# mLSTM values leave their PSUM banks into the tiles of the mLSTM's loads: a decoder block on one core

## The chip, the cores and the metric

The kernel runs on one NeuronCore of a Trainium2 chip, as one program. Five engines work side by side, each through its own queue of instructions: TensorE (PE) multiplies matrices into banks of PSUM, VectorE (DVE) and ScalarE (ACT) work elementwise and read PSUM, GpSimd (POOL) works on SBUF and issues transfers, SyncE (SP) issues transfers. The engines wait for each other by semaphores. The metric is the device time of one execution in microseconds (us).

## What is computed

One decoder block over a sequence of 2048 tokens of width 1024, in float32. Two token mixers run in parallel on one combined projection, followed by a gated FFN:

```python
h = modulate(rms_norm(x, g_pre_mix[l]), shift_m, scale_m)
proj = h @ w_in[l]
q_a, k_a, v_a, q_m, k_m, v_m, o_m, i_m, f_m, g_a, g_m = jnp.split(proj, split_points, axis=-1)
...
y_a = sliding_window_attention(q_a, k_a, v_a, attn_sinks[l]).astype(x.dtype)
...
h_m = mlstm_chunkwise(q_m.reshape(B, S, MLSTM_HEADS, MLSTM_HEAD_DIM),
                      k_m.reshape(B, S, MLSTM_HEADS, MLSTM_HEAD_DIM),
                      v_m.reshape(B, S, MLSTM_HEADS, MLSTM_HEAD_DIM), i_pre, f_pre)
y_m = (jax.nn.sigmoid(o_m.astype(jnp.float32)) * head_layer_norm(h_m, mlstm_norm_w[l])).astype(x.dtype)
merged = jax.nn.sigmoid(g_a) * (y_a @ w_branch_attn[l]) + jax.nn.sigmoid(g_m) * (y_m @ w_branch_mlstm[l])
mix = merged @ w_out[l]
x = x + gate_m[:, None, :] * rms_norm(mix, g_post_mix[l])
h2 = modulate(rms_norm(x, g_pre_ffn[l]), shift_f, scale_f)
ff = (jax.nn.silu(h2 @ w_ffn_gate[l]) * (h2 @ w_ffn_up[l])) @ w_ffn_down[l]
x = x + gate_f[:, None, :] * rms_norm(ff, g_post_ffn[l])
```

Here `v_m`, the mLSTM's values, are 512 columns of the projection (4 heads of 128). They are what the change is about.

## The kernel before

**Tiling.** The sequence is cut into four blocks of 512 tokens (`TB`, numbered 0 to 3), and each block into four token tiles of 128 (`NT`). Two blocks make a superblock: blocks 0 and 1, then blocks 2 and 3. Each matrix product is made of three matmuls per operand pair, since each float32 operand is split into a high and a low part (`mm3`, line 283; ScalarE casts the high part, VectorE subtracts the low part: lines 267 and 268 or 1744 and 1745). The larger products of the projection go by a seven-product scheme over two blocks at once (`pair_parts`, line 1854).

**Stages of a superblock.** The projection goes in this order (`superblock`, line 769): for the first block the attention's queries, then keys, values and mLSTM gates, then the mLSTM's values (`vm`, line 867); for the second block keys and values first, then queries, then the mLSTM's values; then for both blocks the pairs of output gate, mLSTM queries and keys, and branch gates. In block 0 the first products are made by `first_block` in an order written out by hand. Attention, the gates' scan and later the mLSTM's chunks run as streams: Python generators that are spawned with a due time and stepped between matmuls (`tick`, line 231), so their instructions lie between those of the projection.

**A product by token groups.** `token_group` (line 339) takes four PSUM banks, one for each token tile (`acc_tile`, a pool of four banks), and goes through the weights two rows of tiles at a time. In the last step it finishes token tile 0, hands its bank to `evac`, then token tile 1, and so on. The next group takes the same four banks in the same order, so its first matmul into a bank follows the evacuation of that bank.

**The values.** `evac` in `vm` (lines 868 to 871) takes a tile, copies the bank into it on ScalarE (line 870), and stores it to the DRAM tensor `vm_d` by a transfer that SyncE issues (line 871). The mLSTM's chunks read `vm_d` later (line 1084). There are four blocks with four token tiles each: 16 copies and 16 stores.

**The two pools of tiles in question.** `tx` (line 124) gives tiles of a pool with nine buffers, the common temporaries. Its other users around the values are: the copies of the queries' banks and their rotated form (lines 813 and 787), the keys and values of blocks 1 to 3 (line 839) and their rotated form, the pieces of the adaLN weights that SyncE loads (line 475 and 476), and the results of the pairs. A query's or key's tile is given back when its stores to `at_d` have landed, which POOL issues (lines 806, 833, 851 and 853). `ld` (line 735) gives tiles of a pool with four buffers. Its users are the keys and values of block 0 (line 839; the stores of lines 851 and 853 and the transpose of line 827 read them) and the loads of the mLSTM's keys and queries by chunk (line 1078, two tiles for a chunk). A tile is 128 partitions by 512 float32 in both. A user that finds no free buffer waits for the last reader of the oldest one.

**Order.** `first_block` is in program order on the engines. After it (line 1713) the framework's planner, with a simulated time line (`schedule_with_timeline_sim=True`, line 2237), orders each engine's queue at compile time: an instruction whose tile is not yet free in the simulation can be placed behind others that the program lists later. On the chip each engine then takes its queue in that order.

**Lines that are named further on.** Line 212 is every matmul of a product, line 217 every transpose. Lines 569, 575 and 576 reload and split the input's combinations (`hsums`, line 564), lines 985 and 987 copy and mask the attention's scores, line 803 scales the transposed queries, line 829 copies the transposed keys, line 954 loads an attention block's operands, lines 333 and 1908 load weights. Line 90 stands for every instruction of the hand-written part.

Of the kernel before, what the change touches and what calls it, by code (L numbers as in the profile page):

```python
# [19 lines left out]
P = 128  # L20
# [53 lines left out]
def decoder_block(ctx: ExitStack, tc: tile.TileContext, a: dict, out: bass.AP, dbg=None):  # L74
# [39 lines left out]
    def nm(s):  # L114
        uid[0] += 1
        return f"{s}{uid[0]}"
# [7 lines left out]
    def tx(shape, dtype=F32):  # L124
        return tpool.tile(shape, dtype, tag="tx", name=nm("tx"), bufs=9)
# [192 lines left out]
    def kept_weights(name):  # L318

        n = 528 if name == "kv" else 1024  # L320
        for j0 in range(0, 4, 2):
            for j in ((j0,) if name == "kv" else (j0, j0 + 1)):
                def load(j=j):
                    src = W_D[name]
                    if name != "kv" and j % 2:
                        parts = [split_tile(x) for x in ("whi", "wlo")]
                        for i in range(2):
                            nc.sync.dma_start(parts[i].bitcast(F32), src[:, j, i, :])
                        return [parts]
                    m = 2 if name == "kv" else 1  # L330
                    t = wpool.tile([P, RAWC], F32R, tag="raw", name=nm("raw"))
                    v = t[:, :m * 2 * n].rearrange("p (m i c) -> p m i c", m=m, i=2)
                    nc.sync.dma_start(v.bitcast(F32), src[:, j:j + m, :, :])
                    return [[v[:, q, i, :] for i in range(2)] for q in range(m)]
                raw = Raw(load)
                for q in range(2 if name == "kv" else 1):
                    yield raw, q, 2 * (j + q), 2

    def token_group(srcs, nk, n, lhs, evac, pair_heads=False, stagger=1, store=None, kept=False):

        acc = []
        srcs = list(srcs)
        held = []

        def make(si, k0, kc):
            def mms(wt):
                if not acc:
                    acc.extend(acc_tile() for _ in range(NT))
                held.append((wt, k0, kc))
                if len(srcs) - stagger <= si < len(srcs) - 1:  # L350
                    return
                for t in range(NT):
                    for w_, k0_, kc_ in held:
                        for j in range(kc_):
                            kk = k0_ + j
                            mm3(acc[t][:, :n], lhs(kk, t), (w_[0][:, j, :], w_[1][:, j, :]), kk == 0, kk == nk - 1)
                            yield
                    if si == len(srcs) - 1:
                        evac(t, acc[t])
                held.clear()  # L360
            return mms

        for si, (raw, view, k0, kc) in enumerate(srcs):
            if kept:
                def ready(raw=raw, q=view):
                    return tuple(v.rearrange("p (k c) -> p k c", k=2) for v in raw.tile[q])
                yield Part(raw, ready, make(si, k0, kc))
                continue
            part = piece(raw, view, [kc, n], make(si, k0, kc), pair_heads)
            if store:  # L370
                def prep(do=part.prep, si=si, kc=kc):
                    made = do()
                    for i, v in enumerate(made):
                        nc.sync.dma_start(W_D[store][:, si, i, :].rearrange("p (k c) -> p k c", k=kc), v.bitcast(F32))
                    return made
                part.prep = prep
            yield part

    def srcs_rows(w, nk, c0):
        for k0 in range(0, nk, 4):  # L380
            kn = min(4, nk - k0)
            raw = raw_rows(w, k0, kn, c0)
            for j in range(0, kn, 2):
                yield raw, (lambda t, j=j: t[:, j:j + 2, :]), k0 + j, 2
# [350 lines left out]
    def ld(shape, dtype=F32):  # L735
        t = kvp.tile([P, 512], dtype, tag="ld", name=nm("ld"), bufs=4)
        return t.rearrange("p (k c) -> p k c", k=shape[0])
# [31 lines left out]
    def superblock(sb):  # L769
# [3 lines left out]
        def lhs_h(b):  # L773
            def lhs(kk, t):
                return tuple(p_[:, kk % 4, t * P:(t + 1) * P] for p_ in HC[f"{kk // 4 + 1}{b % 2 + 1}"])
            return lhs
# [89 lines left out]

        def vm(b):
            def evac(t, ps):
                v = tx([P, 512])
                A.copy(v, ps)  # L870
                nc.sync.dma_start(vm_d[b][:, t, :], v)
            if b > 1:
                yield from token_group(kept_weights("vm"), KD, 512, lhs_h(b), evac, kept=True)
            else:
                yield from token_group(srcs_rows(w_in, KD, C_VM), KD, 512, lhs_h(b), evac, store="vm" if b else None)
# [1379 lines left out]
```

## Time and profile before

| what | value |
| --- | --- |
| median of three runs | 2659.16 us (2657.73 to 2660.38) |
| the profiled execution, its own time | 2668.66 us |
| its span, first to last instruction | 2667.0 us |
| mean granted clock of TensorE | 0.994 |

All of the trace is from the one profiled execution. A row of a timeline gives the start and the length in us, the engine, the line of the kernel, the operation, what it writes and reads by the program's names, the shapes and how many were merged; in brackets stands how long the engine was idle before it, and what ended that wait. A row of a line gives the count, the shortest, median and longest duration in ns, and first and last start in us. `acc` and `mix` are PSUM banks, `tx` and `ld` tiles of the two pools, `hl`, `whi` and `wlo` split weights, `big` large tiles, `raw` weights as loaded. SPq and POOLq are the queues on which SyncE and POOL issue transfers.

### The profile page before, as it was taken

How to read it: one execution, taken by the hardware profiler on the slowest of the kernel's cores; microseconds unless marked ns; L12 is line 12 of the kernel's file. 1: busy time of each engine (PE TensorE's matmuls, PEld its weight loads, DVE VectorE, ACT ScalarE, POOL GpSimd, SP SyncE). 2: the span in 40 equal slices, each digit the busy share in tenths (PEclk: the TensorE clock that was granted, in tenths of full speed). 3: DMA queues.
4: the chain of work that ended last, by engine and by line, in shares of the span. 5: the costliest groups of instructions: out<-in, count | busy, mean ns of one | idle time of the engine just before them, and what ended most of it. 6: DMA issues, size and time to landing. Idle time of an engine off the chain costs nothing.

```text
span 2667.0 us, 36229 instructions
## 1 busy us (share of the span) xinstructions
PE 2615.5 (98%) x12546; PEld 2145.8 (80%) x12546; DVE 1937.2 (73%) x3758; ACT 1281.9 (48%) x2531; POOL 300.3 (11%) x473
## 2 busy tenths in 40 slices
PE   8999999999989999999999999999999999999998
PEld 6877788888876788888878888888778888888876
DVE  5878887768676988875777777775776767676466
ACT  6656544545654654454643433345554333333444
POOL 0320001101132000210001111110000011001000
PEclk9899999999999999999999999999999999999999
DMA  7785465887787545597765554446675323234556
GB/s 270 255 303 164 135 196 183 291 301 253 262 313 244 166 135 181 183 296 268 220 238 193 184 169 153 163 139 228 213 242 173 111 99 116 90 111 139 199 196 220
DMA packets 327032, 532.97 MB, mean 200 GB/s; under 512 B 23136, under 2 KB 197724, under 8 KB 320064
## 3 DMA queue, kind: packets, MB, share of 16 engines
q1 hardware_dynamic: 287752, 448.45, 50.4%
q0 software_dynamic: 20880, 66.41, 6.6%
q10 hardware_dynamic: 18216, 15.79, 1.9%
q8 instruction: 99, 1.62, 0.2%
q14 instruction: 85, 0.70, 0.1%
HBM read 367.61 MB, written 154.57 MB: 196 GB/s over the span
## 4 chain that ended last, share of the span: by engine, by line
PE 88%; DVE 4%; DMA 3%; ACT 2%; issue 1%; POOL 0%; ACTq 0%; SPq 0%; DVEq 0%; POOLq 0%
PE acc L212 62%; PE mix L212 22%; PE mix L217 2%; PE acc L90 1%; DVE hl L1745 1%; PE mix L90 1%; DMA raw<-as_d 1%; ACT hl L1744 1%; DMA big<-big 0%; DMA raw<-ws_d 0%; DMA raw<-in_w_in_dram 0%; ACT tm L1002 0%; DMA at_d<-tx 0%; DMA raw<-in_w_ffn_down_dram 0%; ACT big L575 0%
## 5 line engine op out<-in xcount | busy, mean ns | idle before, releaser
L212 PE MATMUL acc<-big,hl 128*128 128x512 f32 x3936 | 936.4, 393 | 7.0 <-ACT tx L870 5.4
L212 PEld LDWEIGHTS acc<-big,hl 128*128 128x128 f32 x3936 | 733.8, 188 | 166.4 <-ACT tx L870 5.9
L1744 ACT CAST hl<-raw 128x512 fp32r<-128x512 f32 x732 | 439.9, 621 | 489.6 <-PE acc L212 208.7
L1745 DVE TENSOR_TENSOR hl<-raw,hl 128x512 fp32r<-128x512 f32 x732 | 495.1, 692 | 198.4 <-ACT hl L1744 196.0
L212 PE MATMUL acc<-whi,big 128*128 128x512 f32 (+1 forms) x896 | 281.6, 390 | 3.0 <-ACT tx L870 3.0
L212 PE MATMUL mix<-big,hl 128*128 128x512 f32 x1056 | 263.0, 390 | 1.8 <-ACT hl L1744 1.1
L212 PE MATMUL acc<-hl,hl 128*128 128x512 f32 x1008 | 237.2, 393 | 6.2 <-DVE hl L1745 3.3
L212 PEld LDWEIGHTS mix<-big,hl 128*128 128x128 f32 x1056 | 197.8, 188 | 44.5 <-ACT hl L1744 2.0
L212 PEld LDWEIGHTS acc<-hl,hl 128*128 128x128 f32 x1008 | 187.1, 188 | 51.8 <-DVE hl L1745 8.8
L212 PEld LDWEIGHTS acc<-whi,big 128*128 128x128 f32 x896 | 168.6, 192 | 36.2 <-ACT tx L870 3.4
L212 PE MATMUL mix<-hl,hl 128*128 128x512 f32 x792 | 182.7, 391 | 3.4 <-ACT hl L1744 2.6
L212 PEld LDWEIGHTS mix<-hl,hl 128*128 128x128 f32 x792 | 147.8, 188 | 37.6 <-ACT hl L1744 4.2
L212 PE MATMUL acc<-wlo,big 128*128 128x512 f32 (+1 forms) x448 | 174.4, 389 | 0.0
L212 PE MATMUL acc<-big,whi 128*128 128x512 f32 x512 | 157.3, 393 | 0.0
L268 DVE TENSOR_TENSOR wlo<-raw,whi 128x1024 fp32r<-128x1024 f32 (+1 forms) x76 | 90.8, 1194 | 65.7 <-ACT whi L267 60.2
L267 ACT CAST whi<-raw 128x1024 fp32r<-128x1024 f32 (+1 forms) x76 | 78.4, 1032 | 109.7 <-PE acc L212 103.5
L492 POOL TENSOR_TENSOR rs<-ms,halves 128x1 f32<-128x1 f32 (+1 forms) x56 | 41.3, 744 | 797.8 <-DVE ms L490 750.4
L212 PE MATMUL mix<-hcT4h,hl 128*128 128x512 f32 x352 | 115.6, 389 | 0.7 <-ACT hl L1744 0.7
L212 PE MATMUL acc<-hcT2h,hl 128*128 128x512 f32 x352 | 115.5, 389 | 0.0
L212 PEld LDWEIGHTS acc<-big,whi 128*128 128x128 f32 x512 | 95.3, 188 | 19.3
L212 PEld LDWEIGHTS acc<-wlo,big 128*128 128x128 f32 x448 | 85.8, 192 | 18.0 <-issue 1.2
L212 PE MATMUL acc<-big,wlo 128*128 128x512 f32 x256 | 97.6, 392 | 0.0
(388 smaller groups left out, 3802.3 us busy)
## 6 DMA issues: line engine op xcount, KB each, us to landing
as_d<-w POOLq DMA_DIRECT2D x154, 256.0 KB, 2.5
raw<-in_w_in_dram SPq DMA_DIRECT2D x36, 1024.0 KB, 5.4
raw<-as_d SPq DMA_DIRECT2D x70, 512.0 KB, 3.8
raw<-in_w_ffn_gate_dram SPq DMA_DIRECT2D x22, 1024.0 KB, 6.1
raw<-in_w_ffn_up_dram SPq DMA_DIRECT2D x22, 1024.0 KB, 5.8
raw<-ws_d SPq DMA_DIRECT2D x40, 512.0 KB, 4.6
tx<-in_w_ada_dram SPq DMA_DIRECT2D x64, 256.0 KB, 5.3
g_d<-tx SPq DMA_DIRECT2D x64, 256.0 KB, 2.4
```

Of the source, the lines that this page charges most:

```text
L90: self.last = tc.keep_in_program_order(f(*p, **k)).ins
L212: T.matmul(o, lhsT=lhsT, rhs=rhs, start=start, stop=stop, skip_group_check=resumed)
L217: T.transpose(o, i, ident[:k, :k])
L267: A.copy(hv, src)
L268: V.tensor_tensor(lv, src, hv.bitcast(F32), op=ALU.subtract)
L492: G.tensor_tensor(r[:, :n], ms[:, :n], nhalf[:, :n], op=ALU.pow)
L1744: A.copy(v(hi), src)
L1745: V.tensor_tensor(v(lo), src, v(hi).bitcast(F32), op=ALU.subtract)
```

## The change

In `vm`, the tile into which a bank of values is copied comes from the pool of the mLSTM's loads, `ld`, in all four blocks. The copy and the store stay as they are.

```diff
         def vm(b):
             def evac(t, ps):
-                v = tx([P, 512])
+                v = ld([1, 512])[:, 0, :]
                 A.copy(v, ps)
                 nc.sync.dma_start(vm_d[b][:, t, :], v)
```

`ld` gives a tile of the same size as a view of three dimensions, so the index takes its one row:

```python
def ld(shape, dtype=F32):
    t = kvp.tile([P, 512], dtype, tag="ld", name=nm("ld"), bufs=4)
    return t.rearrange("p (k c) -> p k c", k=shape[0])
```

## The prediction

> **What bounds the kernel now.** I read the page first: its span, its busy times and its chain; then the windows, the rows of line 870, and the timelines around them.
>
> ```profile
> span 2667.0 us, 36229 instructions
> PE 2615.5 (98%) x12546; PEld 2145.8 (80%) x12546; DVE 1937.2 (73%) x3758; ACT 1281.9 (48%) x2531; POOL 300.3 (11%) x473
> ...
> PE 88%; DVE 4%; DMA 3%; ACT 2%; issue 1%; POOL 0%; ACTq 0%; SPq 0%; DVEq 0%; POOLq 0%
> ```
>
> TensorE is busy for 2615.5 of 2667.0 us, and the chain that ended last runs through it for 88% of the span. The change takes no matmul away, so it can gain only in the 51.5 us where TensorE stands. The windows show where that is (the stretch, its length, then busy time and count of PE, PEld, DVE, ACT and POOL, the granted clock, the DMA share and GB/s):
>
> ```profile
> 200.00:750.00 550.00, 549.79 (x2772) 457.30 (x2771) 425.56 (x915) 294.82 (x581) 58.38 (x68) 1.00 0.67 224
> 872.00:1370.00 498.00, 498.00 (x2455) 412.10 (x2455) 390.16 (x794) 266.84 (x520) 43.73 (x40) 1.00 0.63 207
> 1370.00:2667.00 1297.00, 1274.37 (x5609) 1043.73 (x5607) 894.56 (x1468) 539.45 (x985) 126.36 (x222) 1.00 0.50 168
> ```
>
> From 200 to 750 us TensorE stands 0.21 us in all, from 872 to 1370 not at all; there a faster copy is worth nothing. After 1370 runs the FFN, whose tiles come from a pool of its own. What is left lies before 200 us and between 750 and 872, and that is where line 870 runs:
>
> ```profile
> L870 ACT COPY tx<-acc x16: 575/587/596, 95.4 to 870.4; 128x512 f32<-128x512 f32 x16
> ...
>   PE acc L212: 8.4, 4
> ```
>
> TensorE waited for a copy of line 870 four times, 8.4 us in all. That is the whole direct prize, 0.3% of the span. These are the four (idle before, and who ended it, in brackets):
>
> ```profile
> 104.80 0.39 PE L212 MATMUL acc<-whi,big 128*128 128x264 f32 x1 [0.31 <-ACT tx L870]
> ...
> 108.97 0.59 PE L212 MATMUL acc<-whi,big 128*128 128x264 f32 x1 [2.69 <-ACT tx L870]
> ...
> 192.50 1.20 PE L212 MATMUL acc<-big,hl 128*128 128x512 f32 x4 [0.82 <-ACT tx L870]
> ...
> 858.72 1.22 PE L212 MATMUL acc<-big,hl 128*128 128x512 f32 x2 [4.55 <-ACT tx L870]
> ```
>
> Two fall in block 0, one in block 1, none in block 2, one in block 3.
>
> **The change part by part.** Nothing is added or taken away: 16 copies of 587 ns and 16 stores stay, source and shape are the same. What moves is the wait for a free tile: out of the nine common temporaries, into the four of the loads. So each block is asked the same question: does the load tile come free earlier, and what would TensorE wait for next?
>
> *Block 0.* The four load tiles hold the keys and values of block 0 here (line 839). ScalarE's rows:
>
> ```profile
> 98.17 0.63 ACT L267 CAST whi<-raw 128x528 fp32r<-128x528 f32 x1 [1.41 <-PE acc L212]
> 98.71 0.26 ACT L829 CAST tx<-mix 128x128 fp32r<-128x128 f32 x1
> 98.95 1.09 ACT L803 ACTIVATE tx<-mix 128x512 fp32r<-128x512 f32 x2
> 102.09 2.18 ACT L575 CAST big<-big 128x512 fp32r<-128x512 f32 x4 [2.05 <-DMA big<-big]
> 104.18 0.57 ACT L870 COPY tx<-acc 128x512 f32<-128x512 f32 x1
> 108.34 0.59 ACT L870 COPY tx<-acc 128x512 f32<-128x512 f32 x1 [3.58 <-issue]
> 108.82 1.21 ACT L985 COPY tm<-mix 128x256 f32<-128x256 f32 x4
> ```
>
> Copies three and four come at 104.18 and 108.34, behind work that the program lists after them; ScalarE stood 3.58 us before the fourth. The view names no releaser; below is a store of line 833 that landed 0.1 us before, and whose common tile a key stream gives back, so I take it for the one. The last reader of a load tile is line 851, the store of the value difference:
>
> ```profile
> L851 POOL DMA_DIRECT2D at_d<-ld x3: 540/540/549, 79.9 to 84.2; - x3
> ...
> DMA to landing us min/median/max: 2.0/3.0/3.0
> ```
> ```profile
> 98.73 0.73 POOL L833 DMA_DIRECT2D at_d<-tx  x1 [4.69 <-issue]
> 99.46 0.55 POOL L851 DMA_DIRECT2D at_d<-ld  x1
> ```
> ```profile
> L833 POOL DMA_DIRECT2D at_d<-tx x1: 729/729/729, 98.7 to 98.7; - x1
> ...
> DMA to landing us min/median/max: 9.5/9.5/9.5
> ```
> ```profile
> at_d<-ld POOLq DMA_DIRECT2D x1, 64.0 KB, 9.5
> ```
>
> That store of line 833 landed at 98.73 + 9.5 = 108.23. Three load tiles are free by 84.2 + 3.0 = 87.2 us, or once TensorE has transposed their keys, before the copies want them; so copies one to three go when their banks are full and the 0.31 us goes. The fourth load tile's store goes out at 99.46 and lands 9.5 us later, at 108.96. So the fourth copy exchanges one landing for the next one on the same queue, 0.73 us behind. Nothing covers that: TensorE stands from 108.97 - 2.69 = 106.28 for this copy alone. Behind it on ScalarE stand the four score copies of line 985, which move with it; their attention step follows TensorE's key group and shifts as that does. The end of the stall moves from 108.97 to about 109.7. **Block 0: +0.7 us**, the 0.31 us being swallowed by the longer wait behind it.
>
> [...]
>
> ```profile
> 92.00:112.00 20.00, 17.00 (x113) 15.29 (x112) 16.01 (x36) 10.64 (x22) 6.65 (x11) 0.90 0.96 334
> ```
>
> The DMA engines are 96% busy in these 20 us. I take the 9.5 us.
>
> *Block 1.* The load tiles stand idle here: their own loads begin at 374.6 us, and block 1's keys go through common temporaries.
>
> ```profile
> L1079 SPq DMA_DIRECT2D ld<-qk_d x16: 359/371/1361, 374.6 to 1150.4; - x16
> ```
> ```profile
> 191.87 0.58 ACT L870 COPY tx<-acc 128x512 f32<-128x512 f32 x1
> ```
> ```profile
> 188.44 1.28 DVE L1745 TENSOR_TENSOR hl<-raw,hl 128x512 fp32r<-128x512 f32 x2
> ```
>
> The copies go on time, and what TensorE needs beside the bank, the split weights, is done at 189.7. **Block 1: -0.8 us.**
>
> *Block 2.* TensorE named no copy there. Its stop of that stage is
>
> ```profile
> 766.18 2.19 PE L212 MATMUL acc<-raw,big 128*128 128x264 f32 x10 [4.18 <-ACT tm L985]
> ```
> ```profile
> L333 SPq DMA_DIRECT2D raw<-w_kv_d x1: 1462/1462/1462, 752.2 to 752.2; - x1
> ...
> DMA to landing us min/median/max: 13.8/13.8/13.8
> ```
>
> and the operand `raw` landed at 752.2 + 13.8 = 766.0, so no earlier copy shortens it. **Block 2: 0.**
>
> *Block 3.* The largest stall, 4.55 us, carries the copy's name, but:
>
> ```profile
> 857.05 1.14 ACT L1744 CAST hl<-raw 128x512 fp32r<-128x512 f32 x2 [8.55 <-DMA raw<-in_w_in_dram]
> 858.09 1.07 ACT L870 COPY tx<-acc 128x512 f32<-128x512 f32 x2
> ```
> ```profile
> 857.98 1.29 DVE L1745 TENSOR_TENSOR hl<-raw,hl 128x512 fp32r<-128x512 f32 x2
> ```
>
> ScalarE had nothing to do for 8.55 us, until a load of projection weights landed at 857.0; the copy merely stands behind the cast of that load. The matmul at 858.72 reads `hl`, whose low part VectorE writes as the first of two subtractions from 857.98 in 1.29 us, so it is there at about 858.65. With the copy gone from the way, TensorE waits for that. **Block 3: -0.1 us at most, taken as 0**, unless the load itself goes out earlier, which is a rival below.
>
> Two more effects have no row before, since the order of each queue is made by the planner, and are bounded. The common temporaries lose 4 of their users per block: the loads on SyncE that wait for one (row in the rivals) may go out earlier, which is worth 0 to -4.5 us, block 3's stall; and they may be planned into a worse order, worth up to the same to the other side. I take 0, as the nine holders at that wait are the keys' and queries' tiles, which stay. The stores of line 871 go out up to 104.18 - 98.17 = 6 us earlier in block 0, if copy three takes the place of line 267's cast, beside DMA engines 96% busy; 256 KB at the 334 GB/s of that row are 0.8 us on a neighbour's landing, either way.
>
> Sum: +0.7 - 0.8 + 0 + 0 = -0.1 us. The profiled execution took 2668.66 us (span 2667.0), 9.5 us more than the median 2659.16 of the three runs; the sum is a difference, which I set on the median: **2659 us**, with 2656 to 2662 for this case alone.
>
> **The rivals.** *Quick landing* (12%): the fourth tile's store lands like its three siblings, in 3.0 us, because the planner puts it elsewhere on POOL's queue or the earlier value stores change what is in flight. Then copy four goes at 102.5 and block 0 gains 0.31 + 2.69 = 3.0 us: 2659.2 - 3.0 - 0.8 = 2655.4. For it: the three siblings. Against it: its neighbour took 9.5 us too. [...]
>
> *Pulled load* (22%, faster): as well as that, the load behind block 3's stall goes out earlier.
>
> ```profile
> SPq L476 <- DMA at_d<-tx: 29.8, 3, 19.9
> ```
> ```profile
> 841.25 0.33 SPq L476 DMA_DIRECT2D tx<-in_w_ada_dram  x1
> 845.21 0.32 SPq L954 DMA_DIRECT2D at<-at_d  x1
> 845.62 0.40 SPq L1908 DMA_DIRECT2D raw<-in_w_in_dram  x1
> ```
>
> SyncE stood 19.9 us in one wait of the adaLN load for a common temporary, and the weights' load is third behind it. If fewer users of those tiles let the planner put it 845.62 - 841.25 = 4.4 us sooner, the 4.55 us go: 2659.2 - 3.0 - 0.8 - 4.5 = 2650.9.
>
> *Blocked ScalarE* (24%, slower): the planner takes the fourth load tile for free early and puts copy four right behind copy three, at about 98 us. ScalarE works in its order, as its 3.58 us before 108.34 show; it would stand there until 109, and behind it stand lines 267, 829, 803 and 575: 0.63 + 0.26 + 1.09 + 2.18 = 4.2 us that today lie inside the wait. Added to the 0.7 us, and to the weights' split that TensorE then needs (0.63 us cast, some 0.7 us subtraction), that is 6.2 us: 2665. It decides from the point where copy four stands ahead of line 575 on ScalarE. For it: three of four tiles are free, so the planner sees little reason to wait. Against it: the fourth tile's release is planned from the store behind line 833, as today's is.
>
> That the copies do not move at all cannot be: the tile is named in the line.
>
> **How the numbers follow.** The exchange has 42%, quick landing 12%, pulled load 22%, blocked ScalarE 24%. A measurement of this kernel can tell some 0.2% from no change, 5.3 us. Exchange and quick landing lie within it: 54% same. Pulled load is 8.3 us faster: 22%; blocked ScalarE 6 us slower: 24%. The range reaches from the pulled load, 2650, to the blocked ScalarE with one of its neighbours late as well, 2666.
>
> **What would show it.** Right: in block 0 copies one to three follow their matmuls, the fourth still starts at 108 to 110 us, behind the landing of line 851's last store; TensorE's stop there ends at 109 to 110; block 1's stop is gone; block 3's is there with line 1744 or 1745 as its end. Wrong: copy four at 103 or before; line 575 behind it; the load of line 1908 before 842; or any stop of TensorE over 1 us between 200 and 750 or 872 and 1370.

## The result and the profile after

The changed kernel took **2665.62 us** (median of 19 runs, 2663.15 to 2669.97), the kernel before 2661.33 us beside it (19 runs, 2657.73 to 2665.70): a ratio of 1.0015, 95% interval 1.0009 to 1.0021. By the medians it is 4.3 us slower, where no change was forecast. The profiled execution took 2664.18 us. Three single runs among the experiments below, one with block 2 alone (3360 us) and two without block 3 (4387 and 12774 us), were slow ones, and the ratios leave them out.

The page of the changed kernel, with TensorE's busy time and the row of line 870 with what its engine waited for (the view lists nobody who waited for it):

```profile
span 2662.4 us, 36217 instructions
PE 2611.1 (98%) x12546; PEld 2141.9 (80%) x12546; DVE 1943.6 (73%) x3758; ACT 1281.3 (48%) x2531; POOL 300.1 (11%) x473
...
PE 88%; DVE 5%; DMA 4%; ACT 2%; issue 1%; POOL 0%; ACTq 0%; SPq 0%; DVEq 0%; POOLq 0%
```
```profile
L870 ACT COPY ld<-acc x16: 577/585/611, 94.5 to 848.7; 128x512 f32<-128x512 f32 x16
...
  PE acc L212: 7.9, 7
  DMA vm_d<-ld: 0.9, 1
```

The direct prize was collected: no stop of TensorE names line 870 any more. Other names came. Before 200 us, the timeline of TensorE has these three stops (the idle time is in brackets):

```profile
110.79 0.44 PE L217 MATMUL mix<-ident,tm 68*128 68x68 f32 x4 [2.84 <-DVE tm L912]
123.11 0.50 PE L212 MATMUL acc<-whi,big 128*128 128x512 f32 x1 [0.91 <-ACT tx L840]
167.71 0.50 PE L212 MATMUL acc<-wlo,big 128*128 128x512 f32 x1 [0.26 <-DVE wlo L268]
```

The second and the third fall in block 1. The kernel before had in block 1, beside the 0.82 us on line 870, a stop that the prediction does not show:

```profile
187.38 0.66 PE L217 MATMUL mix<-ident,tx 128*128 128x128 f32 x4 [1.22 <-DVE tm L1035]
```

With 0.31, 2.69 and 0.27 us (the last by line 912) in block 0 that is 5.31 us of stops before, against 4.01 us after.

In block 3 one stop of 4.55 us became three. The view of waits from 840 to 950 us (total, times, longest), of the kernel before:

```profile
PE acc L212 <- ACT tx L870: 4.6, 1, 4.6
```

and of the changed kernel:

```profile
PE acc L212 <- ACT hl L1744: 3.3, 1, 3.3
PE acc L212 <- DVE hl L1745: 2.8, 1, 2.8
PE mix L217 <- POOL tm L1005: 2.3, 3, 1.0
PE acc L212 <- ACT big L575: 1.9, 1, 1.9
```

That is 10.3 us against 4.6. What stands between the stops is read from TensorE's timeline, first before, then after:

```profile
853.19 0.98 PE L212 MATMUL mix<-at 64*128 64x256 f32 x12
858.72 7.34 PE L212 MATMUL acc<-big,hl 128*128 128x512 f32 x24 [4.55 <-ACT tx L870]
865.99 1.69 PE L212 MATMUL mix<-at 64*128 64x256 f32 x24
867.61 3.04 PE L212 MATMUL acc<-big,hl 128*128 128x512 f32 x12
870.57 1.32 PE L212 MATMUL mix<-at 64*128 64x256 f32 x12
```
```profile
848.36 6.71 PE L212 MATMUL acc<-big,hl 128*128 128x512 f32 x26 [3.29 <-ACT hl L1744]
856.94 0.59 PE L212 MATMUL acc<-big,hl 128*128 128x512 f32 x1 [1.86 <-ACT big L575]
860.37 9.48 PE L212 MATMUL acc<-big,hl 128*128 128x512 f32 x33 [2.84 <-DVE hl L1745]
869.78 0.98 PE L212 MATMUL mix<-at 64*128 64x256 f32 x12
```

`acc<-big,hl` are the products of the pairs, `mix<-at` the attention's scores. Before, 24 matmuls of the pairs are followed by 24 of the attention, then 12 by 12: while TensorE works on scores, the rows of ScalarE and VectorE show the splits for the next product (lines 575, 576, 1744, 1745; beside the scores from 865.99 to 867.68, line 1745 at 865.97 and 866.80, line 1744 at 866.15). After, 60 matmuls of the pairs come in one row, and 12 score matmuls that stood ahead of the first stop have moved behind them. Three of the splits are then waited for in the open. VectorE's queue adds to that: in the changed kernel the scan of block 3's gates (lines 905 to 912, 4.4 us of work from 852.81 to 859.49) stands between these splits, while before it was over at 854.47, ahead of the splits that start at 857.98. SyncE's queue shows the same turn, before and after:

```profile
845.21 0.32 SPq L954 DMA_DIRECT2D at<-at_d  x1
845.62 0.40 SPq L1908 DMA_DIRECT2D raw<-in_w_in_dram  x1
...
847.48 1.01 SPq L954 DMA_DIRECT2D at<-at_d  x1
...
849.44 2.42 SPq L1908 DMA_DIRECT2D raw<-in_w_in_dram  x1
```
```profile
839.43 0.38 SPq L1908 DMA_DIRECT2D raw<-in_w_in_dram  x1
...
842.62 0.38 SPq L1908 DMA_DIRECT2D raw<-in_w_in_dram  x1
...
853.21 0.34 SPq L954 DMA_DIRECT2D at<-at_d  x1
...
854.14 0.38 SPq L954 DMA_DIRECT2D at<-at_d  x1
```

The weights go out earlier than before, the attention's operands later. The windows give the price with the clock (28 us each; before, then after):

```profile
844.00:872.00 28.00, 23.45 (x131) 18.71 (x130) 21.70 (x43) 13.56 (x29) 3.26 (x6) 0.94 0.89 335
```
```profile
844.00:872.00 28.00, 19.95 (x87) 14.74 (x86) 22.71 (x42) 14.12 (x27) 1.62 (x3) 0.88 0.98 368
```

TensorE works 3.5 us less in the same 28 us, and the mean granted clock falls from 0.94 to 0.88: a half-clock window of 6.8 us (0.12 of 28 us is 3.4 us lost) stands there instead of one of 3.4 us. The DMA engines are busier, 0.98 against 0.89. Two single profiles differ by chance as well, so this is a first reading; the runs below test parts of it.

### The profile page after: what moved, and what is told of

The parts are those of the page before. It is cut to its first block, busy times and chain, and to the rows that moved or that the text cites. A ratio compares the mean times of both kernels' runs of the same rounds, so it can differ in the third digit from the quotient of the medians.

```text
span 2662.4 us, 36217 instructions
## 1 busy us (share of the span) xinstructions
PE 2611.1 (98%) x12546; PEld 2141.9 (80%) x12546; DVE 1943.6 (73%) x3758; ACT 1281.3 (48%) x2531; POOL 300.1 (11%) x473
## 4 chain that ended last, share of the span: by engine, by line
PE 88%; DVE 5%; DMA 4%; ACT 2%; issue 1%; POOL 0%; ACTq 0%; SPq 0%; DVEq 0%; POOLq 0%
PE acc L212 61%; PE mix L212 23%; PE mix L217 2%; PE acc L90 1%; DVE hl L1745 1%; PE mix L90 1%; ACT hl L1744 1%; DMA y_d<-tm 1%; DMA raw<-w_kv_d 1%; DMA raw<-in_w_in_dram 1%; ACT tm L1002 0%; DMA raw<-as_d 0%; DMA raw<-ws_d 0%; DMA tx<-in_w_ada_dram 0%; DMA big<-big 0%
```

## The experiments

The expectations test five theories. A: the loss is made where SyncE stands in a value store of block 3. B: it is made in block 0. C: each block adds a little. Two came later. D: the new order at the start of block 3's pairs is the loss. E: each value in a load tile adds its part.

Times are medians; a ratio is to the runs of before on the same chip in the same sitting (medians 2661.42, 2662.25, 2662.13, 2662.65 and 2662.38 us in the five sittings).

**One block at a time.** Load tiles in block N alone:

```diff
-                v = ld([1, 512])[:, 0, :]
+                v = ld([1, 512])[:, 0, :] if b == N else tx([P, 512])
```

> Only block 0's values go into the load tiles; blocks 1 to 3 keep the common temporaries. Theory A (the loss of about 4 us is made in block 3, where SyncE's queue is planned in another order and the attention's operands are loaded later): within 1.5 us of the kernel before, since block 0's order does not touch block 3. Theory B (the exchange of landings in block 0 is dearer than the +0.7 us forecast, with TensorE's clock lowered after a longer stop): 3 to 5 us slower. Theory C (a little from each block): 1 us slower.

> Only block 1's values go into the load tiles. Theory A: 0 to 1 us faster, the 0.8 us stop of block 1 being gone. Theory B: the same. Theory C: 1 us slower.

> Only block 2's values go into the load tiles. Theories A and B: within 1 us of before, as TensorE's stop of that stage ends with the landing of the key weights. Theory C: 1 us slower.

> Only block 3's values go into the load tiles. Theory A: 3 to 6 us slower, with TensorE's stops at the start of the projection pairs adding up to about 8 us in place of 4.6 us, and two or three stops on line 1005 some 30 us later. Theory B: within 1 us of before. Theory C: 1 us slower.

| load tiles in | median | ratio | 95% interval |
| --- | --- | --- | --- |
| block 0 | 2671.50 | 1.0044 | 1.0030 to 1.0057 |
| block 1 | 2664.07 | 1.0010 | 1.0001 to 1.0019 |
| block 2 | 2664.17 | 1.0011 | 1.0002 to 1.0020 |
| block 3 | 2671.74 | 1.0042 | 1.0029 to 1.0055 |

Each block alone is slower (blocks 1 and 2 barely clear of noise), and the four together would be +26 us, where all at once are +4.3. So a block's price is not a property of its tiles alone. The plans differ too: TensorE's order in blocks 0 and 1 with block 0 alone is neither that of before nor that of the changed kernel, and its order in block 3 with block 3 alone is not that of the changed kernel. None of the theories A to C had that.

**Two blocks at a time** (the condition is `b < 2`, `b > 1`, `b in (1, 2)`):

> Load tiles in blocks 0 and 1 alone. If the loss is made in block 3 (theory A or D): within 1.5 us of before, 2660-2663, since the stops between 92 and 200 us go from 5.3 to about 4.0 us. If it is made in block 0: 2664-2667. If stages add up, this kernel's and the next one's distances from before sum to the +4.3 us of the whole change.

> Load tiles in blocks 2 and 3 alone. If the loss is made in block 3: 2665-2668, with TensorE's stops of 745 to 875 us at 15-18 us and an attention step behind the stop of block 3. If it is made in block 0: 2660-2663. Blocks 0 and 1 are as before there.

> Load tiles in blocks 1 and 2 alone, the two blocks whose profiles had the shortest stops (2.1 us between 92 and 200 us for block 1 alone, 10.5 us between 745 and 875 us for block 2 alone, against 5.3 and 13.3 before). If the stops of one profile tell the time: 2655-2659, the fastest of all. If the medians of the single runs add up instead (+2.7 and +2.8): 2666-2668.

Blocks 0 and 1: 2666.28 (1.0012, 1.0003 to 1.0020). Blocks 2 and 3: 2668.24 (1.0021, 1.0012 to 1.0029). Blocks 1 and 2: 2667.08 (1.0013, 1.0004 to 1.0023). All three are slower, the first two again do not add up (+4.0 and +6.0), and the hope for the third, taken from the stops of two single profiles, fell: single profiles do not tell a time to 3 us.

**Value stores of block 3 off SyncE.**

```diff
-                nc.sync.dma_start(vm_d[b][:, t, :], v)
+                (G if b == 3 else nc.sync).dma_start(vm_d[b][:, t, :], v)
```

> All four blocks take tiles of the loads, as in the changed kernel; only block 3's four value stores go out on POOL's queue instead of SyncE's. TensorE, ScalarE and VectorE keep the changed kernel's order to the last instruction, SyncE's is the same less those four rows. Theory A (the loss of 4 us is made where SyncE stands 7.8 us in block 3's third value store, with the attention's loads of line 954 behind it): the first of these loads goes out before 848 instead of at 853, TensorE's stops between 845 and 875 us fall from 8.0 to about 5 us, the time falls to 2661-2663. Theory D (the loss lies in the new order itself, which puts an attention step behind the stop; what SyncE does is hidden): 2664-2667 as for the changed kernel, the loads of line 954 earlier or not.

2666.86 us (1.0013, 1.0005 to 1.0022), as the changed kernel. The load of line 954 went out at 854.4 us although nothing of block 3's line 871 stood ahead of it: SyncE now stood 5.5 us in an adaLN load (line 476) from 848.79. So the store's 7.8 us are not the loss, and theory A falls as it was stated. Whether an earlier load of line 954 would gain was not tried, as it did not come earlier. The waits from 840 to 950 us show the changed kernel's stops, a little shorter:

```profile
PE acc L212 <- ACT hl L1744: 3.5, 1, 3.5
PE acc L212 <- DVE hl L1745: 2.6, 1, 2.6
PE mix L217 <- POOL tm L1005: 1.9, 3, 0.9
PE acc L212 <- ACT big L575: 1.1, 1, 1.1
```

**The gates of block 0 earlier.**

```diff
-            yield L_GATE
+            yield L_GATE - (1400.0 if b == 0 else 0.0)
```

> The changed kernel with the gates' stream of block 0 due 1.4 us earlier (line 894), which moves two transposes of the gates ahead by a dozen matmuls on TensorE and nothing outside block 0. Theory B (in block 0 TensorE's stop did not go, it changed its owner: the scan of the gates on VectorE, 7.4 us from line 899 to line 912, now ends last): the stop of 2.84 us that names line 912 falls to about 1 us, 0.9 us (its start ahead) plus about 0.7 us (one subtraction of line 576 fewer ahead of it), and the time falls by 1.5 to 3 us, to 2663-2664. Rival (something else is due at the same moment): the stop keeps its length under another name, time as changed, 2665-2666.

2668.98 us (1.0020, 1.0011 to 1.0029), and the stop by line 912 grew to 3.92 us. Theory B as stated falls, and POOL's and VectorE's timelines say why. Of this kernel:

```profile
106.58 0.73 POOL L833 DMA_DIRECT2D at_d<-tx  x1 [4.09 <-issue]
107.30 1.68 POOL L806 DMA_DIRECT2D at_d<-tx  x3
108.97 0.54 POOL L907 MEMSET tm<- 68x512 f32 x1
```
```profile
109.54 0.68 DVE L910 TENSOR_TENSOR tm<-tm,tm 4x512 f32<-4x512 f32 x1
```

and of the changed kernel:

```profile
105.88 0.73 POOL L833 DMA_DIRECT2D at_d<-tx  x1 [4.34 <-issue]
106.60 1.64 POOL L806 DMA_DIRECT2D at_d<-tx  x3
108.23 0.54 POOL L907 MEMSET tm<- 68x512 f32 x1
```
```profile
108.81 0.68 DVE L910 TENSOR_TENSOR tm<-tm,tm 4x512 f32<-4x512 f32 x1
```

Line 910 writes into the tile that POOL clears in line 907, and starts 0.03 to 0.04 us after that clearing ends, in both (108.97 + 0.54 = 109.51; 108.23 + 0.54 = 108.77). The clearing stands on POOL behind the stores of block 0's keys and queries, which POOL issues after standing 4 us. So the chain that ends TensorE's stop in block 0 is not the scan but POOL's queue of stores, and an earlier scan gains nothing. Whether an earlier clearing would gain was not tried.

**Block 3 left out.** The condition is `b < 3`; the two kernels were run again beside it, unchanged.

> Load tiles in blocks 0 to 2, common temporaries in block 3, so that the order of block 3 from its last stop on is that of before. If the loss of the whole change is made in block 3's order: no stop by line 1005 after 875 us, stops of 745 to 875 us at 10-13 us, time 2660-2663. If it comes from block 0 as the run with blocks 0 and 1 (+4.0) suggests: 2664-2667.

> The changed kernel once more, for its granted clock in every run and a second profile. The kernel before lost 0.45% of its clock in the mean of its runs, 12.0 us at half of it. Theory D (the new order makes more and longer stops, and each stop over 2 us is followed by a half-clock window of 3.4 us or a multiple): 0.50-0.55% lost, 13.5-14.5 us, so about half of the 4 us is clock and half stops; the stops of 745 to 875 us come to 15-18 us again, those of 92 to 200 us to 4-5 us. Rival (the windows are chance, the same for both): 0.45% lost.

> The kernel before, a second profile. Its first one fell 7 us above its median, with a half-clock window of 13.7 us from 107.8 us on. Expected: the same stops within 1 us in the stretch of 92 to 200 us (5.3), 10-13 us in that of 745 to 875 us, none between 875 and 1370; a shorter window in block 0, and a span of 2657-2662.

Without block 3: **2662.22 us, ratio 0.9996 (0.9987 to 1.0005)**. The changed kernel again: 2666.48 (1.0018, 1.0009 to 1.0026). So blocks 0 to 2 together make no difference that can be measured, and taking block 3 back takes the whole loss back. That holds for this plan only: with block 2 taken back as well (blocks 0 and 1 above) the median is 2666.28 again. The changed kernel's second profile has stops of 3.59, 0.83 and 2.91 us in block 3; before's second profile one of 4.57 us there and none between 875 and 1370, as its first. Its half-clock window in block 0 was 13.7 us again. The mean granted clock of this sitting was 0.9958 before, 0.9954 without block 3 and 0.9943 for the changed kernel. Each run's time by what its clock lacks to 1 gives 11.2, 12.1 and 15.3 us lost to half clock. The mean times less that loss are 2651.1, 2649.4 and 2651.1 us, so from blocks 0 to 2 to all four 3.2 us were lost to half clock and 1.7 us beside it. In other sittings the losses were 11.5 to 12.1 us before, 13.6 without block 3 and 14.3 for the changed kernel, so how the loss divides is known only roughly.

**One or two of block 3's values.** Load tiles in blocks 0 to 2, and in block 3 for some of the four token tiles:

```diff
-                v = ld([1, 512])[:, 0, :]
+                v = ld([1, 512])[:, 0, :] if b < 3 or t == 0 else tx([P, 512])
```

(`t == 0` here, then `t >= 2`, then `t == 3`, with the second and the kernel without block 3 repeated)

> Load tiles in blocks 0 to 2 and for the first of block 3's four values only. The plan then has the flipped order of the changed kernel in block 3: on SyncE the attention's loads of line 954 stand behind both weight loads of line 1908, and on TensorE 12 score matmuls of the attention have moved from ahead of the first pair's matmul to 36 behind it (before: the next step 24 behind). Theory D (that order costs the time): 2665-2668, stops by lines 575 and 1745 after the first one of block 3, stops by line 1005 after 875 us. Rival E (each value in a load tile adds its part, by the tiles themselves): about a quarter of the 4 us, 2663.

> Load tiles in blocks 0 to 2 and for the last two of block 3's values. Here the plan keeps the order of before up to block 3's pairs: lines 954 ahead of 1908 on SyncE, all 108 score matmuls ahead of the first pair's matmul, the next step 24 behind. Theory D: as without block 3, 2661-2664, no stop by line 1005 after 875 us. Rival E: half of the 4 us, 2664-2665.

> Load tiles in blocks 0 to 2 once more, as the reference of the two runs beside it, for its median and a profile that can be read: 2661-2663, the stops of 745 to 875 us at 10-14 us, none after 875.

> Load tiles in blocks 0 to 2 and for the last of block 3's values only. TensorE, VectorE and POOL get the very order that they have with the last two values in load tiles; on ScalarE and SyncE only one copy and one store stand elsewhere. If the order alone makes the loss of +3.5 us over the run without block 3: the same again, 2665-2667. If each tile adds its part: half of it, 2663.5-2664.5.

> The last two of block 3's values in load tiles once more, beside the run with one, for a second profile. If its loss is in the order behind the pairs' first product: stops by line 1005 between 875 and 950 us again (2.4 us of stops there in its first profile, none without block 3), time 2665-2667.

| values of block 3 in load tiles | order in block 3 | median | ratio | 95% interval |
| --- | --- | --- | --- | --- |
| none | as before | 2662.71 | 0.9998 | 0.9989 to 1.0006 |
| the first | turned at the pairs' start | 2666.18 | 1.0012 | 1.0004 to 1.0021 |
| the last | kept there, other behind | 2665.51 | 1.0014 | 1.0005 to 1.0023 |
| the last two | the same | 2666.16 | 1.0009 | 1.0000 to 1.0018 |
| the last two, again | the same | 2664.17 | 1.0011 | 1.0002 to 1.0020 |
| all four (above) | turned | 2666.48 | 1.0018 | 1.0009 to 1.0026 |

One value costs as much as four: Rival E, a price per tile, falls. But Theory D as it stood falls too, since the last two values cost 1.5 to 3.5 us over the run without block 3, although the order at the pairs' start was kept. The run with the last value alone has the very same order on TensorE, VectorE and POOL as that with the last two, and loses 2.8 us over the run without block 3, between their two results. What it waits for from 840 to 950 us, against the kernel without block 3:

```profile
PE acc L212 <- ACT tx L870: 4.1, 1, 4.1
PE mix L217 <- POOL tm L1005: 2.0, 2, 1.4
PE acc L212 <- ACT tx L1896: 0.6, 1, 0.6
```
```profile
PE acc L212 <- ACT tx L870: 4.9, 1, 4.9
```

The stop at the pairs' start is still there under the same name; three more stand behind it, in two rows. TensorE's timeline at the first of them, with the last value in a load tile, and without block 3:

```profile
884.65 0.60 PE L217 MATMUL mix<-ident,tm 128*128 128x128 f32 x4
886.69 1.66 PE L217 MATMUL mix<-ident,tm 128*128 128x128 f32 x12 [1.44 <-POOL tm L1005]
```
```profile
886.58 0.60 PE L217 MATMUL mix<-ident,tm 128*128 128x128 f32 x4
887.14 2.57 PE L212 MATMUL acc<-big,hl 128*128 128x512 f32 x10
889.54 1.04 PE L217 MATMUL mix<-ident,tm 128*128 128x128 f32 x8
890.34 3.02 PE L212 MATMUL acc<-big,hl 128*128 128x512 f32 x12
893.19 0.60 PE L217 MATMUL mix<-ident,tm 128*128 128x128 f32 x4
```

The same 16 transposes of softmax weights, each group of which needs a product of POOL (line 1005): here twelve of them come in one row and wait 1.44 us, there they lie between products of the pairs and don't wait.

**Where the time goes, over all profiles.** The start of TensorE's n-th matmul, counted along the trace, cuts every profile at the same work, up to a dozen matmuls that a plan moves over a mark. Time in us between marks; in brackets the stops and the time lost to half clock:

```
load tiles in           400-2000 (blocks 0, 1)  3500-4200 (block 2)  4200-5000 (block 3, first pairs)
none                    314.7 (5.5 + 6.8)       123.6                158.2 ( 5.0 + 1.7)
none, again             313.2 (4.3 + 6.8)       124.5                158.3 ( 5.0 + 1.7)
0                       316.0 (7.6 + 1.7)       122.5                157.2 ( 4.6 + 1.7)
1                       306.4 (2.5 + 1.7)       123.5                159.9 ( 5.2 + 3.4)
2                       312.3 (5.1 + 5.1)       123.4                155.3 ( 3.8 + 1.7)
0, 1                    310.2 (4.7 + 1.7)       123.2                161.3 ( 6.9 + 3.4)
1, 2                    308.0 (3.9 + 1.7)       123.6                160.4 ( 8.0 + 3.4)
0, 1, 2 (again)         311.5 (4.4 + 3.4)       121.9                159.8 ( 7.1 + 3.4)
0 to 2, last of 3       311.1 (4.4 + 3.4)       122.3                162.9 ( 9.0 + 3.4)
0 to 2, last two of 3   311.1 (4.2 + 3.4)       124.2                162.2 ( 7.5 + 3.4)
the same, again         310.7 (4.0 + 3.4)       123.4                162.4 ( 7.6 + 3.4)
0 to 2, first of 3      310.3 (3.7 + 3.4)       121.5                164.3 ( 9.8 + 6.8)
all                     309.6 (4.0 + 1.7)       123.3                163.2 (10.5 + 3.4)
all, again              310.9 (4.1 + 3.4)       121.5                163.4 ( 9.2 + 5.1)
all, block 3 by POOL    312.3 (5.2 + 3.4)       121.7                163.0 ( 9.5 + 3.4)
all, gates earlier      310.7 (4.9 + 3.4)       125.8                162.9 ( 8.5 + 5.1)
3                       310.4 (5.4 + 1.7)       127.2                166.8 (10.7 + 6.8)
2, 3                    310.7 (5.8 + 1.7)       123.8                164.1 (13.1 + 5.1)
```

Between 2000 and 3500 every kernel took 302.2 us. The last column separates: 155.3 to 161.3 us in the eight profiles without a load tile in block 3, 162.2 to 166.8 in the ten with one or more. Profiles in which TensorE has the very same order agree in it within 1.4 us: 162.9 to 163.4 for the changed kernel's order (four profiles), 162.2 to 162.9 for that with the last one or two values (three), 159.8 and 160.4 for blocks 0 to 2 and blocks 1 and 2, 159.9 and 161.3 for block 1 and blocks 0 and 1. From blocks 0 to 2 to all four it is 159.8 to 163.3, **+3.5 us**, against 4.3 and 3.8 us between the medians of these two kernels (2662.22 and 2662.71 against 2666.48).

The other columns say less. In the first, the five profiles with before's order on TensorE reach from 310.4 to 314.7 us, so the difference of 1.4 us between their mean (312.3) and that of the ten with both blocks changed (310.8) lies within the scatter of one order. And the mark at 4200 is not the same work in all plans: with load tiles in block 2, nine matmuls of a product stand ahead of it in place of nine of the attention's scores, by their rows some 1.3 us more work. From 3500 to 5000 in one stretch it is 281.8 and 282.8 us before, 281.7 without block 3, 286.5 and 284.9 for the changed kernel. So beyond matmul 3500 nothing is lost without block 3, which fits the 0.0 of that run, and some 3 to 5 us with it.

## Why the prediction was wrong

**The failed step** is the term for the planner: "they may be planned into a worse order, worth up to the same to the other side. I take 0, as the nine holders at that wait are the keys' and queries' tiles, which stay." The order did change, in every queue (in POOL's only by three instructions at 126 us), and with the new order of block 3 came +3.5 us. The bound of 4.5 us held, the reason for taking its middle was not: it looked at who holds the tiles in which SyncE waits, not at what else the planner may lay out anew once the values are free to leave early.

The distance to the forecast has a second part. The forecast of 2659 us lies 6.6 us under the 2665.62 measured, and 2.2 of these come from its base: the median of three runs, 2659.16, lay that far under the 2661.33 of 19 runs.

Point by point:

- **What bounds it.** Right: TensorE's stops are what changed, and their place before 200 and between 750 and 872 us held but for 2.3 us by line 1005 at 889 to 941 us, where before had none (0.89, 0.99 and 0.45 us, just under the 1 us that was named as a sign of error). Left out were the stops by other lines, as the 1.22 us by line 1035.
- **Block 0, +0.7.** Not borne out, in mechanism or size. The stops in block 0 were 0.31 + 2.69 us on line 870 and 0.27 on line 912, 3.27 us; after, 2.84 us on line 912. In the second profiles it is the other way, 2.13 + 0.18 before and 3.23 after, so one pair of profiles does not tell the sign. Copies one to three did follow their matmuls. The fourth went at 103.82, not at 108 to 110:

```profile
103.82 0.58 ACT L870 COPY ld<-acc 128x512 f32<-128x512 f32 x1 [0.93 <-DMA vm_d<-ld]
```

```profile
95.11 2.24 SPq L871 DMA_DIRECT2D vm_d<-ld  x3
```
```profile
vm_d<-ld SPq DMA_DIRECT2D x3, 256.0 KB, 8.6
```

  The releaser is a store of line 871: the fourth copy took the tile that the first value had left, whose store went out at 95.11 and landed 8.6 us later, at 103.7. It exchanged one landing for another, but not for that of the fourth key, so the 9.5 us on which the step rested never came into it. What was late next was POOL's queue, 2.84 us.
- **Block 1, -0.8.** The 0.82 us by line 870 is gone in both profiles of the changed kernel, as forecast. So is the 1.22 us by line 1035, which was not forecast, and 0.91 us by line 840 came new in both (beside 0.26 us in the first), so the stops fell from 2.04 to 1.17 us: the size is near by luck.
- **Block 2, 0.** Its stop held, 4.18 and 4.28 us before, 4.29 and 3.75 after. Another, 2.64 us by line 987, is gone, and smaller ones came (0.73, 0.84, 1.11 and 0.39 us in the first profile).
- **Block 3, 0.** Wrong by 3.4 us of stops in the first pair of profiles (3.29 + 1.86 + 2.84 = 7.99 for 4.55) and 2.8 in the second (3.59 + 0.83 + 2.91 = 7.33 for 4.57). The step held that line 1745 would end the same stop. It did end one, but on a later operand, while line 1744 ended the first; before, the attention's matmuls stood ahead of such later operands.
- **Quick landing (12%).** The last store of line 851 landed after 6.9 us, neither 3.0 nor 9.5, and copy four did not wait for it.
- **Pulled load (22%).** Its cause came: line 1908 went out at 839.43, before the 842 that was named as its sign. Its gain did not. On SyncE it now stands ahead of the attention's loads, and the score matmuls that covered the next splits stand later too.
- **Blocked ScalarE (24%).** Its time, 2665 us, is the one measured; its mechanism is not: copy four stood behind line 575, and TensorE did not wait for it. That the time agrees is luck.
- **Left out of the sum: the clock.** Every stop was priced at its own length. Half-clock time goes with most long stops (63 of 67 of 2 us or more, below), and the changed kernel lost 14.3 and 15.3 us so in the means of its two sets of runs, against 11.2 to 12.1 before: 2 to 4 us of the loss by this count.

**What stays open.** How the loss divides between stops and half clock is not settled. In the last column, from blocks 0 to 2 to all four, the stops grow by 2.7 us, and half-clock time in which TensorE works costs 0.8 us more (the part of a window that falls into a stop is not counted: in the changed kernel TensorE is busy for 3.99 of the 6.83 us from 857.20), together the 3.5 us; the runs' clocks gave 0.7 to 3.2 us to half clock. The two profiles of before lost some 16 us to half clock in all (clock 0.994), above the 11.2 to 12.1 us of its runs in the mean, so they are slower than the kernel usually is. Why single blocks cost more than all together (block 0 alone +10 us) was not settled either; in its one profile block 0 alone shows 316.0 us from matmul 400 to 2000 against 312.3 in the mean of before's order, 3.7 of the 10. And the tiles cannot be exchanged without a new plan, so the price of the old order with the new tiles was not measured: that the step from blocks 0 to 2 to all four brings the loss is shown, that the order makes it is argued from the profiles. Where blocks 0 and 1 alone lose their 4.0 us is not known. No version was clearly faster than the kernel before.

## What to carry to other kernels

Where a planner orders the queues at compile time, changing the pool of a tile changes the program, not one wait: compare the order of every queue before and after, and look for work that lay between a load and its use and has moved. A stop that is taken away can show what was due behind it (in the first profiles of block 0 the 2.69 us by line 870 made way for 2.84 us by line 912), so ask of every stop which operand is next and what covers it. And leave out one part at a time from the full change: parts that were added one at a time cost +26 us here, the whole cost +4.

## What the hardware showed that was not expected

**Half clock goes with stops of 2 us.** TensorE's granted clock is 1.0 or 0.5 in these traces, and the half-clock windows up to 2650 us last 3.4 us or a multiple (3.41, 6.83 and 13.65 us in the first profiles of the two kernels). In each profile they begin on one grid of 3.41 us (in the first one of before at 53.21, 107.82, 766.60 and 858.76 us: 16, 193 and 27 steps apart). In the 18 profiles above, between 90 and 2650 us, 63 of 67 stops of 2 us or more have such a window that begins in them, at most 1 us ahead or 4 us behind, or that runs already when they begin (6 of 8 in the first profiles of the two kernels); of 275 stops of 0.6 to 2 us, 12 have one. Under a busy TensorE each 3.4 us window is 1.7 us of work lost: before, the windows view counts 8 matmuls from 858.76 to 862.17 us, at a clock of 0.50, and 16 in the next 3.41 us, at 1.00. From these counts I estimate that a stop of 2 us costs nearly 4 (2 + 1.7) where its window falls behind it, and that two stops of 1.5 us would cost less than one of 3; no run tried that. Stops of 2 to 3 us, shorter than a window, had one in 24 of 27 cases.

**A clearing can stand behind stores on POOL's queue.** POOL's 0.54 us for line 907 ended a stop of 2.84 us of TensorE, since it stood behind four stores that POOL had to issue, the first after 4.34 us in which the profile shows no releaser. The view of TensorE's waits names only the last of that chain, line 912.
